# Attention scores of a head pair in one three-bank PSUM tile, with one maximum per head, from the 21st pair on

## The chip, the cores and the metric

The kernel runs on one core of one Trainium2 chip. The metric is device time in microseconds (us) of one launch; the result is the median of several launches.

## What is computed

Two layers of a diffusion backbone run over 1024 latent tokens of width 1024, beside 256 context tokens. Layer 0 mixes tokens with a gated MLP, layer 1 with windowed attention, and a ConvGLU feed-forward follows each. The change lies in the attention of layer 1: blocks of 128 queries, 16 heads of 64 dimensions, 4 key/value heads. Cut to what matters:

```python
scale = HEAD_DIM ** -0.5
for j in blocks:                        # 8 blocks of 128 queries
    s_lat = q[j] @ k[j-1 : j+2].T       # up to three key blocks
    s_lat = where(|q - k| <= 128, s_lat * scale, -inf)
    s_ctx = q[j] @ k_ctx.T * scale      # all 256 context keys
    p = softmax(concat(s_lat, s_ctx, sink))   # the sink column is dropped after
    out[j] = p_lat @ v[j-1 : j+2] + p_ctx @ v_ctx
y = out @ w_o
```

Blocks 1 to 6 have 384 local keys and 256 context keys (640 in all), blocks 0 and 7 have 256 and 256.

## The kernel before

One program is written as if for a single thread; a scheduling layer then places each engine's instructions in a fixed order and adds the semaphores. Every engine works through its queue in that order, so an instruction that waits holds up all that stand behind it on its engine. All instructions are recorded in one helper, so the profile gives L50 as the line of nearly everything; groups are told apart by the names of the tiles that they write and read.

Large matmuls are done in three passes of a high and a low part ("wh", "wl" and so on). Attention (`att_a`, `att_b`, `att_c`, lines 1876 to 1968) is a software pipeline over 64 pairs of heads, numbered i = 8 j + 2 g + pr for block j, key/value head g and pair pr. The loop at line 2028 issues, for each i, `att_a` of pair i (scores, maximum, softmax), `att_b` of pair i - 2 (transposes of the softmax weights) and `att_c` of pair i - 3 (weights times values). From i = 20 on it also weaves in steps of the output projection (`o_steps`, line 1970), by the table `sched`: six 512-column matmuls a step, named "wh,oc" in the profile.

- `att_a`: TensorE multiplies the queries of a head ("tmp") with the keys' high and low parts ("big"). The sign is folded in, so the maximum is a minimum. On VectorE a masked add with a running minimum (CUSTOM_DVE_ANT_0) moves scores from PSUM to SBUF, into `Pt` ("tmp" for the first head, "wl" for the second), and a READ_ACCUMULATOR writes the minimum to "sm". ScalarE then takes the exponential with that bias and adds up the row, VectorE takes the reciprocal, and GpSimd (POOL) multiplies.
- Pairs 8 to 23 are "merged": each head has its own two-bank tile `psA` with context and local scores side by side, six matmuls, and one VectorE operation over 640 columns.
- All other pairs put both heads' local scores in one `psA` tile (a bank each) and both heads' context scores in one bank `psB`: eight matmuls, then four VectorE operations, since a second one per head carries the minimum on over the context.
- `att_b`: ten 128-column transposes ("ident,tmp" and "ident,wl") into three `psB` banks; ScalarE casts a bank to "act" (high part), and VectorE subtracts to get the low part.
- `att_c`: ten 256-column matmuls ("act,y") into one `psB` bank, then a ScalarE copy and two VectorE adds into "row".

PSUM has eight banks: two buffers `psA` of two banks and four buffers `psB` of one, for the whole program. While an output projection is under way, one `psA` holds its sum `pacc` for eight steps, and scores have the other.

Of the kernel before, what the change touches and what calls it, by code (L numbers as in the profile page):

```python
# [10 lines left out]
F32 = mybir.dt.float32  # L11
F32R = mybir.dt.float32r
AF = mybir.ActivationFunctionType
ALU = mybir.AluOpType

P = 128
D = 1024
KD = D // P
# [14 lines left out]
def hybrid_kernel(  # L33
# [37 lines left out]
    open_pool("mix")  # L71
    ps = ctx.enter_context(tc.tile_pool(name="ps", bufs=1, space=bass.MemoryType.PSUM))
    dr = ctx.enter_context(tc.tile_pool(name="dr", bufs=1, space=bass.MemoryType.DRAM))
# [3 lines left out]
    def nm(s):  # L77
        uid[0] += 1
        return f"{s}_{uid[0]}"
# [43 lines left out]
    def t_sm(w=2):  # L123
        return sb.tile([P, w], F32, name=nm("sm"), tag="sm", bufs=24)
# [5 lines left out]
    def psA(shape=(P, 2, 512)):  # L130
        return ps.tile(list(shape), F32, name=nm("psA"), tag="psA", bufs=2)

    def psB(shape=(P, 512)):
        return ps.tile(list(shape), F32, name=nm("psB"), tag="psB", bufs=4)

# [43 lines left out]
    ones = ones_r.bitcast(F32)  # L179
    mhalf = const.tile([P, 1], F32, name="mhalf")  # L180
    G.memset(mhalf, -0.5)
    mone = const.tile([P, 2], F32, name="mone")
    G.memset(mone, -1.0)
# [242 lines left out]
    def tick():  # L426
        for gen in list(active):
            if next(gen, 1):
                active.remove(gen)
# [393 lines left out]
    def gmlp(si, hb, tiles, gate, extra, between, pre_last, on_flip=None, head=None, order=(0, 1, 2, 3, 4), mod=None):  # L823
        st = const.tile([P, 5, 24], F32, name=nm("st"))
        if head:
# [28 lines left out]
        rs, nmr = t_sm(5), t_sm(5)  # L854
        mv = t_sm(10).rearrange("p (i n) -> p i n", i=5)
        for i in range(5):
# [960 lines left out]
    def after_b(bi, u):  # L1817
# [9 lines left out]
        if bi == 2:  # L1827
# [5 lines left out]
            if u == 2:  # L1833
                q_prep(0, 1)

    maskw = const.tile([P, 640], F32, name="mask")
    G.memset(maskw, 0.0)
# [4 lines left out]
                    pattern=[[-1, 384]], channel_multiplier=1)  # L1842
    NM = 24
    snk = const.tile([P, NH], F32, name="snk")
# [28 lines left out]
    def merged(j, g, pr):  # L1873
        return 8 <= 8 * j + 2 * g + pr < NM

    def att_a(j, g, pr):
        k0, kts = geo[j]
# [9 lines left out]
        if merged(j, g, pr):  # L1887
            for h in range(2):
                lh = qs[:, 2 * pr + h, :]
                sl = psA()  # L1890
                for dst, c in ((sl[:, 0, 0:256], 1024), (sl[:, 0, 256:512], k0 * P), (sl[:, 1, 0:P], k0 * P + 256)):
                    n = dst.shape[-1]
                    T.matmul(dst, lh, KH[g][:, c:c + n], start=True, stop=False)
                    T.matmul(dst, lh, KL[g][:, c:c + n], start=False, stop=True)
                V.tensor_tensor_reduce(out=Pt[h][:, 0:NK], in0=sl.rearrange("p a b -> p (a b)")[:, 0:NK],
                                       in1=maskw[:, 0:NK], scale=1.0,
                                       scalar=nsnk[:, h0 + h:h0 + h + 1], op0=ALU.add, op1=ALU.min,
                                       accum_out=mx[:, h:h + 1])
            softmax(Pt, mx, es, dn, h0, NK)
            at[(j, g, pr)] = Pt  # L1900
            return
# [22 lines left out]
    def att_b(j, g, pr):  # L1924
        nk = len(geo[j][1])
        Pt = at[(j, g, pr)]
        PTh, PTl = t_act((P, 5, 2, P)), t_act((P, 5, 2, P))
        for a in range(0, nk, 2):
            n = min(2, nk - a)
            pt = psB((P, 2, 2, P))  # L1930
            for b in range(n):
                for h in range(2):
                    T.transpose(out=pt[:, b, h, :], in_=Pt[h][:, (a + b) * P:(a + b + 1) * P], identity=ident)
            S.copy(PTh[:, a:a + n], pt[:, 0:n])
            V.tensor_sub(PTl[:, a:a + n], pt[:, 0:n], PTh[:, a:a + n])
        at[(j, g, pr)] = (PTh, PTl)
# [3 lines left out]
    def att_c(j, g, pr):  # L1940
        kts = geo[j][1]
        nk = len(kts)
        if merged(j, g, pr):
            kts = kts[-2:] + kts[:-2]
# [25 lines left out]
    def o_steps(tiles):  # L1970
# [22 lines left out]
        for h in range(2):  # L1993
            pacc = psA()
            for k in range(KD):
                load(h * KD + k + 2)
                w, oc = wts.pop(h * KD + k), ocs.pop(h * KD + k)
                for i in range(nt):
                    hs = slice(i * P, (i + 1) * P)
                    mm3(pacc[:, i, :], oc[:, 0, hs], oc[:, 1, hs], w[:, 0], w[:, 1],  # L2000
                        k == 0, k == KD - 1)
                yield
            for i in range(nt):
                S.copy(ys[i][:, h * 512:(h + 1) * 512], pacc[:, i, :])
        for i in range(nt):
# [21 lines left out]
    n_pairs = len(pairs)  # L2027
    for i in range(n_pairs + LC):
        if i < n_pairs:
            j, g, pr = pairs[i]  # L2030
# [26 lines left out]
    while next(og, 1) is None:  # L2057
        tick()

    def last_o():  # L2060
# [20 lines left out]
    lat_ffn(1, 3, 5, halos, gate_of(1, 5), chain(last_o(), flushes(True)), ada_steps(1, 5, (0,), True))  # L2081
    stage_pool["guard"].__exit__(None, None, None)


# [40 lines left out]
```

## Time and profile before

| what | value |
|---|---|
| median of three runs | 2849.98 us (2846.95 to 2852.19) |
| the profiled execution, its own time | 2852.14 us |
| its span, first to last instruction | 2850.4 us |
| mean granted TensorE clock | 0.990 |
| TensorE matmul (PE) busy | 2735.4 us (96%) |
| VectorE (DVE) busy | 2218.6 us (78%) |
| ScalarE (ACT) busy | 1390.8 us (49%) |
| GpSimd (POOL) busy | 623.2 us (22%) |
| scores of pair 20 begin, last scores of pair 63 end | 1879 us, 2129 us |

How to read it: spans and starts count from the first instruction. A matmul's end is modelled, and neighbours overlap, so for TensorE the step from one start to the next says more than the duration. "PEld" is the weight load of a matmul. An entry "[1.29 <-DVE sm]" is idle time ahead of an instruction with the engine and tile that ended it.

### The profile page before, as it was taken

What the parts mean: (1) busy time and instruction counts of PE and PEld (TensorE: products, weight loads), DVE (VectorE), ACT (ScalarE), POOL (GpSimd) and SP (SyncE); (2) the same over time, 40 slices, a digit from 0 to 9 for tenths busy, and PEclk for the clock granted to TensorE, in tenths of its full rate; (3) what the DMA queues carried; (4) which work ended last, traced back from release to release, by engine and by line L of the source; (5) the groups of instructions that cost most, each with busy time, mean ns of one, the idle gap of its engine ahead of it and who ended that gap; (6) DMA issues with size and microseconds to landing.
All of it is one profiled execution on the core that took longest, in us unless ns stands there. A gap on an engine that the chain in (4) does not pass through costs nothing.

```text
span 2850.4 us, 40321 instructions
## 1 busy us (share of the span) xinstructions
PE 2735.4 (96%) x14570; PEld 2348.8 (82%) x14570; DVE 2218.6 (78%) x3466; ACT 1390.8 (49%) x2291; POOL 623.2 (22%) x806
## 2 busy tenths in 40 slices
PE   7999999999989999999999999899998999999998
PEld 5798887898879888888888788788887888888886
DVE  6567685687779898887786658898887788888776
ACT  4233243232367444455444545777876444445433
POOL 1064021260110122121000124543332122220000
PEclk9999999999999999999999999999999999999999
DMA  7785447554478345467845665347577355445753
GB/s 261 237 244 171 146 142 240 184 158 127 174 233 249 121 159 170 143 219 231 313 157 187 201 210 188 115 139 238 186 241 231 122 168 179 157 144 196 254 176 125
DMA packets 436335, 537.13 MB, mean 188 GB/s; under 512 B 20004, under 2 KB 300452, under 8 KB 436135
## 3 DMA queue, kind: packets, MB, share of 16 engines
q1 hardware_dynamic: 379575, 470.84, 51.5%
q10 hardware_dynamic: 55408, 59.52, 6.2%
q0 software_dynamic: 1152, 4.19, 0.4%
q8 instruction: 115, 1.88, 0.3%
q14 instruction: 85, 0.70, 0.1%
HBM read 414.40 MB, written 120.07 MB: 188 GB/s over the span
## 4 chain that ended last, share of the span: by engine, by line
PE 69%; DVE 12%; DMA 9%; ACT 4%; issue 4%; POOL 2%; SPq 1%; ACTq 0%; DVEq 0%; POOLq 0%
PE psB L50 52%; PE psA L50 17%; DVE row L50 3%; DMA raw<-in_ada_w_dram 3%; DVE wl L50 3%; DVE acc L50 1%; DVE tmp L50 1%; ACT wh L50 1%; DVE y L50 1%; ACT tmp L50 1%; DMA raw<-in_f_w_up_dram 1%; DMA xT<-row 1%; SPq L50 1%; POOL sm L50 1%; DVE act L50 1%
## 5 line engine op out<-in xcount | busy, mean ns | idle before, releaser
L50 PE MATMUL psB<-cmb,wh 128*128 128x512 f32 (+2 forms) x2584 | 750.5, 374 | 8.1 <-ACT row L50 5.6
L50 PEld LDWEIGHTS psB<-cmb,wh 128*128 128x128 f32 x2584 | 471.9, 188 | 99.2 <-ACT row L50 8.0
L50 PE MATMUL psB<-cmb,wl 128*128 128x512 f32 (+2 forms) x1292 | 482.9, 374 | 0.0
L50 ACT CAST wh<-raw 128x1024 fp32r<-128x1024 f32 (+1 forms) x313 | 265.2, 863 | 436.4 <-PE psB L50 173.6
L50 DVE TENSOR_TENSOR wl<-raw,wh 128x1024 fp32r<-128x1024 f32 (+1 forms) x313 | 308.9, 1002 | 97.2 <-ACT wh L50 95.5
L50 PEld LDWEIGHTS psB<-cmb,wl 128*128 128x128 f32 x1292 | 243.1, 188 | 43.6 <-DVE wl L50 0.2
L50 PE MATMUL psB<-wh,big 128*128 128x512 f32 x816 | 271.4, 399 | 4.0 <-ACT big L50 1.3
L50 ACT CAST wh<-row 128x1024 fp32r<-128x1024 f32 (+1 forms) x196 | 162.5, 834 | 189.9 <-DVE row L50 97.0
L50 PE MATMUL psB<-wh,act 128*128 128x512 f32 x640 | 200.2, 391 | 0.8 <-DVE tmp L50 0.8
L50 POOL TENSOR_TENSOR row<-raw,raw 128x512 f32<-128x512 f32 x44 | 73.2, 1664 | 572.2 <-DMA raw<-in_f_w_up_dram 516.6
L50 PE MATMUL psA<-big,wh 128*128 128x320 f32 x1024 | 194.4, 312 | 0.3 <-ACT row L50 0.3
L50 DVE TENSOR_TENSOR wl<-row,wh 128x1024 fp32r<-128x1024 f32 (+1 forms) x196 | 185.4, 949 | 11.8 <-ACT wh L50 11.8
L50 DVE SCALAR_TENSOR_TENSOR acc<-raw,ccols,acc 128x1024 f32<-128x1024 f32 x98 | 125.8, 1302 | 81.2 <-DMA raw<-in_ada_w_dram 81.1
L50 PEld LDWEIGHTS psB<-wh,big 128*128 128x128 f32 x816 | 154.7, 191 | 40.2 <-ACT big L50 2.4
L50 DVE SCALAR_TENSOR_TENSOR row<-row,cwcols,row 128x1024 f32<-128x1024 f32 (+2 forms) x142 | 150.8, 1062 | 39.2 <-ACT row L50 22.6
L50 ACT CAST ah<-raw 128x1024 fp32r<-128x1024 f32 x80 | 77.6, 974 | 202.2 <-PE psB L50 80.9
L50 POOL TENSOR_SCALAR row<-row,sm,sm 128x128 f32<-128x128 f32 x160 | 146.0, 926 | 114.0 <-DMA row<-vscr 63.3
L50 DVE TENSOR_TENSOR row<-row,row 128x512 f32<-128x512 f32 (+4 forms) x169 | 156.9, 932 | 17.3 <-DMA row<-actd 10.5
L50 PEld LDWEIGHTS psA<-big,wh 128*128 128x128 f32 x1024 | 160.9, 189 | 0.7 <-ACT row L50 0.5
L50 PE MATMUL psB<-wl,big 128*128 128x512 f32 x408 | 157.9, 397 | 0.6 <-DVE wl L50 0.6
L50 DVE TENSOR_TENSOR al<-raw,ah 128x1024 fp32r<-128x1024 f32 x80 | 90.3, 1128 | 71.4 <-ACT ah L50 71.1
L50 PE MATMUL psB<-row,wh 128*128 128x256 f32 x744 | 133.6, 283 | 9.5 <-ACT wh L50 7.5
(279 smaller groups left out, 6210.7 us busy)
## 6 DMA issues: line engine op xcount, KB each, us to landing
raw<-in_f_w_up_dram SPq DMA_DIRECT2D x121, 512.0 KB, 4.9
raw<-in_ada_w_dram SPq DMA_DIRECT2D x88, 512.0 KB, 4.4
raw<-in_a_w_in_dram SPq DMA_DIRECT2D x64, 512.0 KB, 4.6
wh<-woscr SPq DMA_DIRECT2D x48, 512.0 KB, 4.4
row<-actd SPq DMA_DIRECT2D x44, 512.0 KB, 5.3
actc<-row SPq DMA_DIRECT2D x44, 512.0 KB, 4.1
raw<-actc SPq DMA_DIRECT2D x40, 512.0 KB, 3.8
actd<-row SPq DMA_DIRECT2D x39, 512.0 KB, 2.6
```

The lines of the kernel that those rows point to most:

```text
L50: ins = fn(*a, **kw)
```

## The change

From pair 20 on (`NM` falls from 24 to 20, so merged pairs are 8 to 19) a pair is "joined": both heads' scores lie in one tile `psS` of three banks. The first head has its 384 local scores at the end of the first bank and its context in the first half of the middle bank; the second head has its context in the second half of the middle bank and its local scores in the third. Each head's 640 columns are so contiguous, and one VectorE operation takes them. The mask gains 256 zero columns at its end, and the transposes of the first head are read in an order that fits.

The PSUM pool is closed and reopened at i = 20 with other sizes: one `psS` (three banks), one `psO` (two banks, for the output projection's sum) and three `psB`. After the projection of the first six blocks it is reopened once more as at the start. The copies out of the projection's sum move into the step that ends it. Two constants now share a tile, and the statistics of layer 0 share another; near 170 us some small VectorE operations change places.

```diff
     def psA(shape=(P, 2, 512)):
-        return ps.tile(list(shape), F32, name=nm("psA"), tag="psA", bufs=2)
+        return banks_pool["pool"].tile(list(shape), F32, name=nm("psA"), tag="psA", bufs=2)
+
+    def psS():
+        return banks_pool["pool"].tile([P, 1536], F32, name=nm("psS"), tag="psS", bufs=1)
+
+    def psO():
+        return banks_pool["pool"].tile([P, 2, 512], F32, name=nm("psO"), tag="psO", bufs=1)
 
     def psB(shape=(P, 512)):
-        return ps.tile(list(shape), F32, name=nm("psB"), tag="psB", bufs=4)
+        return banks_pool["pool"].tile(list(shape), F32, name=nm("psB"), tag="psB", bufs=banks_pool["small"])
...
-    maskw = const.tile([P, 640], F32, name="mask")
+    maskw = const.tile([P, 896], F32, name="mask")
...
-    NM = 24
+    NM = 20
...
+    def joined(j, g, pr):
+        return 8 * j + 2 * g + pr >= NM
...
+        if joined(j, g, pr):
+            sl = psS()
+            for h in range(2):
+                lh = qs[:, 2 * pr + h, :]
+                local, o = (512 - NL, 512 - NL) if h == 0 and j < 7 else (512 * h + 512, 512 * h + 256)
+                context = 512 if h == 0 and j < 7 else 512 * h + 256
+                for c, k, n in ((local, k0 * P, NL), (context, 1024, 256)):
+                    T.matmul(sl[:, c:c + n], lh, KH[g][:, k:k + n], start=True, stop=False)
+                    T.matmul(sl[:, c:c + n], lh, KL[g][:, k:k + n], start=False, stop=True)
+                m = 256 if h == 0 and j < 7 else 0
+                V.tensor_tensor_reduce(out=Pt[h][:, 0:NK], in0=sl[:, o:o + NK], in1=maskw[:, m:m + NK], scale=1.0,
+                                       scalar=nsnk[:, h0 + h:h0 + h + 1], op0=ALU.add, op1=ALU.min,
+                                       accum_out=mx[:, h:h + 1])
+            softmax(Pt, mx, es, dn, h0, NK)
+            at[(j, g, pr)] = Pt
+            return
...
-            pacc = psA()
+            pacc = psO()
...
+                if k == KD - 1:
+                    for i in range(nt):
+                        S.copy(ys[i][:, h * 512:(h + 1) * 512], pacc[:, i, :])
                 yield
-            for i in range(nt):
-                S.copy(ys[i][:, h * 512:(h + 1) * 512], pacc[:, i, :])
...
+        if i == NM:
+            open_banks("ps2", reuse_waits="tile")
+            banks_pool["small"] = 3
...
+    open_banks("ps3", reuse_waits="tile")
```

What this does to the order of instructions is shown at one place, pair 32 and its neighbours, on the two engines that pass the scores on. First TensorE before: "psA" is the tile of local scores and "psB" with "big" that of the context, "tmp" behind "big" the queries; "ident" rows are the transposes of an earlier pair.

```order
L50 MATMUL psA_18022<-big_15607,tmp_17943 128x384
L50 MATMUL psA_18022<-big_15608,tmp_17943 128x384
L50 MATMUL psB_18023<-big_15607,tmp_17943 128x256
L50 MATMUL psB_18023<-big_15608,tmp_17943 128x256
L50 MATMUL psA_18022<-big_15607,tmp_17943 128x384
L50 MATMUL psA_18022<-big_15608,tmp_17943 128x384
L50 MATMUL psB_18023<-big_15607,tmp_17943 128x256
L50 MATMUL psB_18023<-big_15608,tmp_17943 128x256
L50 MATMUL psB_18043<-ident,tmp_17859 128x128
```

The same place on TensorE in the changed program, with the semaphores that instructions wait for; nine transposes (eight of them left out here) stand between the two heads.

```order
L50 MATMUL psS_17979<-big_15604,tmp_17903 128x384 [waits DVE_49]
L50 MATMUL psS_17979<-big_15605,tmp_17903 128x384
L50 MATMUL psS_17979<-big_15604,tmp_17903 128x256
L50 MATMUL psS_17979<-big_15605,tmp_17903 128x256
...
L50 MATMUL psS_17979<-big_15604,tmp_17903 128x384 [waits DVE_49]
L50 MATMUL psS_17979<-big_15605,tmp_17903 128x384
L50 MATMUL psS_17979<-big_15604,tmp_17903 128x256
L50 MATMUL psS_17979<-big_15605,tmp_17903 128x256
```

The eight matmuls came in one piece; now each head's four stand apart, and the second head's first matmul waits for VectorE. Then VectorE before, at the same pair ("ISA" with a mask is the masked minimum, "ISA sm" the read of the accumulator, "act" the low parts of an earlier pair's transposes):

```order
L50 ISA tmp_18018,sm_18016<-psA_18022,mask,nsnk 128x384
L50 ISA sm_18016 128x1
L50 ISA wl_18019,sm_18016<-psA_18022,mask,nsnk 128x384
L50 ISA sm_18016 128x1
L50 ISA tmp_18018,sm_18016<-psB_18023,mask,sm_18016 128x256
L50 ISA sm_18016 128x1
L50 ISA wl_18019,sm_18016<-psB_18023,mask,sm_18016 128x256
L50 ISA sm_18016 128x1
L50 TENSOR_TENSOR act_18042<-psB_18043,act_18041 128x512
```

and in the changed program:

```order
L50 ISA tmp_17975,sm_17973<-psS_17979,mask,nsnk 128x640
L50 ISA sm_17973 128x1
L50 TENSOR_TENSOR act_17996<-psB_17997,act_17995 128x512
L50 ISA wl_17976,sm_17973<-psS_17979,mask,nsnk 128x640
L50 ISA sm_17973 128x1
L50 TENSOR_TENSOR act_17996<-psB_18004,act_17995 128x512
```

Four minima and four reads became two and two, and a subtraction of the transposes moved in between the heads.

More of the change, by code (lines that the diff above doesn't have):

```diff
@@ L71, in hybrid_kernel, with open_banks @@
     open_pool("mix")
-    ps = ctx.enter_context(tc.tile_pool(name="ps", bufs=1, space=bass.MemoryType.PSUM))
+    banks_pool = {}
+    def open_banks(name, **kw):
+        if banks_pool:
+            banks_pool.pop("guard").__exit__(None, None, None)
+        banks_pool["guard"] = tc.tile_pool(name=name, bufs=1, space=bass.MemoryType.PSUM, **kw)
+        banks_pool["pool"] = banks_pool["guard"].__enter__()
+        banks_pool["small"] = 4
+    open_banks("ps")
     dr = ctx.enter_context(tc.tile_pool(name="dr", bufs=1, space=bass.MemoryType.DRAM))
@@ L179, in hybrid_kernel @@
     ones = ones_r.bitcast(F32)
-    mhalf = const.tile([P, 1], F32, name="mhalf")
+    powers = const.tile([P, 3], F32, name="powers")
+    mhalf, mone = powers[:, 0:1], powers[:, 1:3]
     G.memset(mhalf, -0.5)
-    mone = const.tile([P, 2], F32, name="mone")
     G.memset(mone, -1.0)
@@ L823, in gmlp @@
     def gmlp(si, hb, tiles, gate, extra, between, pre_last, on_flip=None, head=None, order=(0, 1, 2, 3, 4), mod=None):
-        st = const.tile([P, 5, 24], F32, name=nm("st"))
+        stats = const.tile([P, 184], F32, name=nm("st"), tag="st")
+        st = stats[:, 0:120].rearrange("p (i n) -> p i n", i=5)
         if head:
@@ L854, in gmlp @@
         rs, nmr = t_sm(5), t_sm(5)
-        mv = t_sm(10).rearrange("p (i n) -> p i n", i=5)
+        mv = stats[:, 120:130].rearrange("p (i n) -> p i n", i=5)
         for i in range(5):
@@ L1932, in att_b @@
                 for h in range(2):
-                    T.transpose(out=pt[:, b, h, :], in_=Pt[h][:, (a + b) * P:(a + b + 1) * P], identity=ident)
+                    c = (a + b + 3) % 5 if h == 0 and nk == 5 and joined(j, g, pr) else a + b
+                    T.transpose(out=pt[:, b, h, :], in_=Pt[h][:, c * P:(c + 1) * P], identity=ident)
             S.copy(PTh[:, a:a + n], pt[:, 0:n])
@@ L1942, in att_c @@
         nk = len(kts)
-        if merged(j, g, pr):
+        if merged(j, g, pr) or joined(j, g, pr):
             kts = kts[-2:] + kts[:-2]
@@ L2082, in hybrid_kernel @@
     stage_pool["guard"].__exit__(None, None, None)
+    banks_pool["guard"].__exit__(None, None, None)
 _INS = ['x', 'c', 'ctx', 'c_ctx', 'ada_w', 'ada_b', 'norm_g', 'a_w_in', 'a_ln_g', 'a_ln_b', 'a_w_s', 'a_b_s',
```

## Prediction

> **What bounds the kernel now.** I read the page's busy times first, then the stretch of the changed pairs.
>
> ```profile
> PE 2735.4 (96%) x14570; PEld 2348.8 (82%) x14570; DVE 2218.6 (78%) x3466; ACT 1390.8 (49%) x2291; POOL 623.2 (22%) x806
> ```
>
> TensorE is busy nearly throughout, so the kernel can only shrink where TensorE idles or does less. The next view cuts the stretch of pairs 20 to 63 into parts, with the busy time of each engine; its last row is the whole stretch, from a second answer.
>
> ```profile
> core 0: us, PE busy (x) PEld busy (x) DVE busy (x) ACT busy (x) POOL busy (x), PEclk, DMA share, GB/s
> 1879.00:1925.00 46.00, 43.16 (x301) 38.26 (x300) 43.65 (x130) 33.02 (x77) 21.23 (x24) 1.00 0.69 221
> 1925.00:1965.00 40.00, 39.44 (x275) 35.70 (x275) 35.14 (x127) 30.07 (x74) 12.55 (x18) 1.00 0.60 200
> 1965.00:1990.00 25.00, 19.70 (x116) 16.80 (x115) 18.66 (x53) 15.11 (x35) 5.85 (x10) 0.93 0.82 273
> 1990.00:2062.00 72.00, 70.41 (x502) 64.01 (x502) 63.53 (x232) 58.69 (x136) 26.45 (x36) 1.00 0.56 187
> 2062.00:2080.00 18.00, 15.43 (x87) 13.14 (x86) 14.82 (x39) 11.43 (x27) 4.62 (x8) 0.91 0.89 296
> 2080.00:2131.00 51.00, 50.50 (x363) 45.62 (x362) 44.26 (x168) 40.56 (x93) 17.95 (x26) 1.00 0.71 242
> ...
> 1879.00:2131.00 252.00, 238.63 (x1634) 213.53 (x1633) 220.07 (x744) 188.86 (x435) 88.64 (x120) 0.99 0.67 223
> ```
>
> TensorE is idle for 252.00 - 238.63 = 13.4 us of the stretch. In 1925 to 1965, 1990 to 2062 and 2080 to 2131, 163 us, it idles 0.56 + 1.59 + 0.50 = 2.65 us: there it sets the pace. The rest lies in three pieces, at the start, where VectorE is busy 43.65 of 46 us, and around 1975 and 2070. Who ended that idle time is told by the waits of TensorE over the stretch.
>
> ```profile
> PE psB L50 <- DVE sm L50: 4.8, 5, 1.6
> PE psA L50 <- DMA oc<-oscr: 2.6, 1, 2.6
> PE psA L50 <- DVE sm L50: 2.3, 4, 1.0
> PE psB L50 <- DVE act L50: 1.9, 3, 0.8
> PE psB L50 <- ACT tmp L50: 0.4, 2, 0.2
> PE psB L50 <- DVE row L50: 0.3, 1, 0.3
> ```
>
> "DVE sm" is the read of a maximum: a bank of scores came free only then. It accounts for 7.1 us, over half. The largest of these is not a score matmul but the values' product, which wanted a `psB` bank that scores still held:
>
> ```profile
> 2017.10 1.08 PE L50 MATMUL psB<-act,y 128*128 128x256 f32 x7 [1.57 <-DVE sm L50]
> ```
>
> **The change part by part.** First the work that VectorE is rid of. The rows of one pair as it is, a pair with 384 local keys:
>
> ```profile
> 1945.60 0.62 DVE L50 CUSTOM_DVE_ANT_0 tmp<-psA,mask,nsnk 128x384 f32<-128x384 f32 x1 [0.43 <-PE psA L50]
> 1946.14 0.08 DVE L50 DVE_READ_ACCUMULATOR2_ANT sm<- 128x1 f32 x1
> 1946.14 0.61 DVE L50 CUSTOM_DVE_ANT_0 wl<-psA,mask,nsnk 128x384 f32<-128x384 f32 x1
> ...
> 1946.68 0.48 DVE L50 CUSTOM_DVE_ANT_0 tmp<-psB,mask,sm 128x256 f32<-128x256 f32 x1
> ...
> 1947.08 0.48 DVE L50 CUSTOM_DVE_ANT_0 wl<-psB,mask,sm 128x256 f32<-128x256 f32 x1
> ...
> 1947.49 1.61 DVE L50 TENSOR_TENSOR act<-psB,act 128x512 fp32r<-128x512 f32 x3
> ```
>
> and of a merged pair, whose two operations have the form that all pairs now get:
>
> ```profile
> 1867.98 0.87 DVE L50 CUSTOM_DVE_ANT_0 tmp<-psA,mask,nsnk 128x640 f32<-128x640 f32 x1
> ...
> 1868.78 0.88 DVE L50 CUSTOM_DVE_ANT_0 wl<-psA,mask,nsnk 128x640 f32<-128x640 f32 x1
> ...
> 1869.59 0.21 DVE L50 COPY wl<-nsnk 128x1 f32<-128x1 f32 x2
> ```
>
> From start to start four operations take 1947.49 - 1945.60 = 1.89 us and two take 1869.59 - 1867.98 = 1.61 us, reads included. So 0.28 us goes with each of pairs 24 to 63. Pairs 56 to 63 have 512 columns: the step of 256 is 1947.08 - 1946.68 = 0.40 us and that of 384 0.54 us, which puts 512 at 0.67 us, and 4 x 0.40 - 2 x 0.67 is 0.26 us, much the same. In all 40 x 0.28 = 11.2 us of VectorE go. Pairs 20 to 23 had one operation a head already. This is a relief of VectorE, not of the path: where TensorE sets the pace it is worth nothing.
>
> TensorE's own work hardly changes. Pairs 24 to 63 keep eight matmuls of the same widths. Pairs 20 to 23 have eight in place of twelve, with the same 640 columns a head; twelve took 1.50 us in the first row below, and eight take 1945.79 - 1944.38 = 1.41 us in the two after it. At most 0.1 us a pair: I take 0.
>
> ```profile
> 1879.02 1.50 PE L50 MATMUL psA<-big,tmp 128*128 128x256 f32 x12
> 1881.51 0.78 PE L50 MATMUL psA<-big,tmp 128*128 128x256 f32 x5 [0.99 <-DVE sm L50]
> ...
> 1944.38 0.60 PE L50 MATMUL psA<-big,tmp 128*128 128x384 f32 x2
> ...
> 1945.39 0.40 PE L50 MATMUL psB<-big,tmp 128*128 128x256 f32 x2
> 1945.63 0.27 PE L50 MATMUL psB<-ident,tmp 128*128 128x128 f32 x1
> ...
> 1946.61 0.27 PE L50 MATMUL psB<-ident,wl 128*128 128x128 f32 x1
> ```
>
> The new wait is the heart of the change. All score matmuls of a pair could go in one piece; now the second head's wait until VectorE has read the first head's maximum, and the next pair's first head waits for the second's, as there is only one `psS`. Behind a waiting matmul stand the rest of the transposes, the values' product and the projection, so each such wait is TensorE's own time. The second row above prices it with nothing in between: the scores of pair 20 ended at 1880.52, the next could start 0.99 us later. The modelled end lies 1945.79 - 1945.63 = 0.16 us behind the slot of the next instruction, so the hand-over costs 1.15 us less the work that stands between. Ten transposes step over (1946.61 - 1945.63) / 9 x 10 = 1.09 us, nine over 0.98 and eight over 0.87. In the changed order only 15 of the 44 first hand-overs have such little work between: one has five transposes (0.60 us short), six have nine (0.17 each), four have ten (0.06 each), three of the 512-column pairs have eight (their maximum is 0.13 us shorter, so 1.02 us is needed and each is 0.15 short) and one has enough. Sum: 0.60 + 1.02 + 0.24 + 0.45 = 2.3 us. Eight more have 1.2 to 1.35 us between and would wait only if VectorE came late. The second hand-over has the values' product and mostly projection work between, but VectorE takes a subtraction of an earlier pair first; I add 1.0 us for the few with the product alone. So 3.3 us; the lower bound is 0 if the queue's own gaps swallow them, the upper one stands with the rivals.
>
> [...]
>
> What goes in return: the 2.3 us of "psA <- DVE sm" vanish as such, since that hand-over is now the one just priced. Of the 4.8 us of "psB <- DVE sm", `psB` no longer holds scores, but with three buffers the values' product takes the bank of that pair's first transposes, whose subtraction follows the first head's maximum on VectorE. That is 0.81 us for the maximum and 0.68 us for the subtraction
>
> ```profile
> L50 DVE TENSOR_TENSOR act<-psB,act 128x512 fp32r<-128x512 f32 x88 | 57.4, 684 | 2.1 <-ACT act L50 1.9
> ```
>
> against 1.89 us, so 0.40 us sooner in each of five waits: 2.0 us. The three waits on "DVE act" come 0.28 us sooner each, 0.8 us. The wait on the load of "oc" stays at 2.6 us, because it hangs on a store and a load of the projection's input.
>
> Parts with one answer, taken at 0: the wider memset on POOL at the start, the shared constants and statistics (the same operations, a few swapped), and swaps of a few loads on SP's queue. The copies out of `psO` are the same pieces on ScalarE,
>
> ```profile
> L50 ACT COPY acc<-psA 128x512 f32<-128x512 f32 x10 | 6.0, 595 | 0.1
> ```
>
> two to a half of the sum; matmuls of attention stand ahead of the next half's, and without that cover five turns would cost up to 1.2 us each. Reopening the pool lets a tile wait for the tiles it overlays only, once each way.
>
> The clock: TensorE had 0.93 and 0.91 of it in the two stretches with the most idle, 25 x 0.07 = 1.8 us and 18 x 0.09 = 1.6 us lost, and 1.00 elsewhere. I leave both. [...]
>
> Sum against the profiled execution: 2852.14 - 2.3 - 2.0 - 0.8 + 3.3 = 2850.3 us. That execution lies 2.2 us above the median, 2849.98, so on the median's scale 2848 us. The three runs spread over 5 us, about 0.2%, which is what counts as a difference here.
>
> **The rivals.** Faster: VectorE's lateness, not the hand-over, is what TensorE pays for, and 11.2 us less of it clears the idle. Of the 13.4 us of idle all but the load's 2.6 us and 0.8 us of small gaps go, which is 10.0 us, and 1.6 us of clock, less 1.0 us of second hand-overs. 2852.14 - 10.6 = 2841.5, or 2839 on the median's scale. For it speaks the first part, where VectorE is busy 43.65 of 46 us; against it that 163 us of the stretch hold 2.65 us of idle.
>
> Slower: the hand-overs bind. VectorE is busy 220 of 252 us, so a first maximum seldom starts at once; if it starts 0.3 to 0.4 us late on average, 23 hand-overs cost about 0.5 us each. 11.5 + 1.0 - 2.3 - 2.0 - 0.8 = +7.4, so 2859.5, or 2857 on the median's scale. For it speaks that the old order issued both heads at once and idled little. It decides from (2.3 + 2.0 + 0.8 - 1.0) / 23 = 0.18 us a hand-over on.
>
> No change: the waits just pass to another tile of the same late engine, since three `psB` are left; 2850.
>
> **How the numbers follow.** My forecast has a chance of 0.42, with 2842 to 2852 as its own range; the faster rival 0.22, the slower 0.18, no change 0.18. Faster by over 0.2% (below 2844.3) takes 0.13 of the forecast, 0.20 of the faster rival and 0.01 of no change: 0.34. Slower takes 0.16 of its rival and 0.02 of no change: 0.18. The rest, 0.48, is the same. The range reaches from just below the faster rival, 2837, to 2858.
>
> **What would show it.** VectorE's busy time should fall by some 11 us by steps (more by durations), with 80 masked minima less. Ahead of "psS" matmuls there should be idle time ended by "DVE sm", a few us in all, and none of it ahead of "psB". If TensorE's idle in the stretch falls to about 4 us, the faster rival holds; if "psS <- DVE sm" sums to 8 us or more, the slower one. A change of more than 3 us outside 1879 to 2190 us would mean that I looked in the wrong place.

## The result and the profile after

The changed kernel takes 2868.22 us (median of 4 runs, 2866.80 to 2870.07), the kernel before 2850.51 us beside it (2846.95 to 2852.19). The ratio is 1.0065, with a 95% interval of 1.005 to 1.008: 17.7 us slower. Its profiled execution took 2866.80 us, with a span of 2865.0 us; the two traces are thus 14.7 us apart and show a little less than the medians.

From the page of the changed kernel, the busy times:

```profile
PE 2745.7 (96%) x14554; PEld 2355.8 (82%) x14554; DVE 2210.7 (77%) x3306; ACT 1392.4 (49%) x2291; POOL 620.2 (22%) x806
```

VectorE has 160 instructions less, the 80 minima and 80 reads, and 7.9 us less to do. It did not help. The stretch of pairs 20 to 63, cut at about the same places of the work as for the kernel before (the last row, from a second answer, is the whole):

```profile
core 0: us, PE busy (x) PEld busy (x) DVE busy (x) ACT busy (x) POOL busy (x), PEclk, DMA share, GB/s
1876.00:1927.00 51.00, 45.84 (x301) 40.01 (x298) 45.37 (x122) 34.84 (x80) 20.54 (x25) 0.97 0.67 213
1927.00:1970.00 43.00, 41.70 (x284) 37.01 (x282) 34.19 (x97) 31.57 (x74) 13.75 (x18) 1.00 0.54 173
1970.00:1992.00 22.00, 17.42 (x98) 14.93 (x99) 16.75 (x39) 13.88 (x33) 5.72 (x8) 0.92 0.93 319
1992.00:2068.00 76.00, 73.09 (x506) 64.67 (x504) 62.27 (x179) 59.47 (x138) 27.51 (x36) 1.00 0.55 179
2068.00:2090.00 22.00, 18.83 (x101) 16.48 (x102) 15.74 (x37) 11.93 (x27) 7.03 (x9) 0.84 0.91 300
2090.00:2142.00 52.00, 50.80 (x350) 44.43 (x350) 40.50 (x118) 40.08 (x93) 17.64 (x26) 1.00 0.61 204
...
1876.00:2142.00 266.00, 247.69 (x1634) 217.51 (x1632) 214.82 (x588) 191.78 (x441) 92.19 (x121) 0.97 0.64 211
```

The stretch grew from 252 to 266 us. TensorE idles 18.3 us in it, where it was 13.4; VectorE idles more than before, 51 us against 32. The waits of TensorE over the same stretch:

```profile
PE psO L50 <- DMA oc<-oscr: 4.8, 2, 2.7
PE psS L50 <- DVE sm L50: 3.7, 7, 1.0
PE psS L50 <- DVE row L50: 3.4, 1, 3.4
PE psB L50 <- ACT tmp L50: 2.4, 4, 1.0
PE psB L50 <- DVE act L50: 1.6, 4, 0.7
PE psB L50 <- DVE row L50: 0.8, 3, 0.3
PE psB L50 <- ACT act L50: 0.3, 1, 0.3
```

"psB <- DVE sm" and "psA <- DVE sm", 7.1 us before, are gone. In their place stand `psS` (7.1 us), a second wait for "oc" and small waits of `psB`. But idle time explains only 4.9 of 14 us, since a matmul's modelled end covers short waits (0.17 us of one in the pair shown below, where its row has no idle time). So all matmul starts of the loop (from the values' product of pair 16 to that of pair 63) were taken instead: the step from each start to the next, less about the shortest step that a matmul of its width has in these two traces at a granted clock of 1.00 (0.226 us for 512 columns, 0.170 for 384, 0.1135 for 256, 0.109 for a transpose; gaps under 0.05 us left out). What is left, by the matmul that came late; steps of about twice their length have a row of their own:

| us of gaps ahead of | before | after |
|---|---|---|
| scores | 6.2 | 17.2 |
| transposes and values' products (`psB`) | 12.2 | 14.7 |
| the projection | 7.1 | 8.1 |
| steps of about twice their length | 8.2 | 7.6 |
| sum | 33.7 | 47.6 |
| this part of the loop | 260.1 | 273.6 |

Without the gaps, both kernels take the same to within 0.4 us (260.1 - 33.7 and 273.6 - 47.6). So the 13.5 us are gaps, most of them (11.0 us) ahead of scores. The row of doubled steps is not the clock alone: by the granted clock in the two views, the stretch lost 25 x 0.07 + 18 x 0.09 = 3.4 us before and 51 x 0.03 + 22 x 0.08 + 22 x 0.16 = 6.8 us after. At least 4.8 of the 8.2 us before are therefore short waits, and the clock takes about 3.4 us more than it did.

The gaps are of three kinds. The first is one wait, at the reopened pool. TensorE of the changed kernel:

```profile
1876.19 1.43 PE L50 MATMUL psB<-act,y 128*128 128x256 f32 x10
1881.00 1.41 PE L50 MATMUL psS<-big,tmp 128*128 128x384 f32 x4 [3.38 <-DVE row L50]
1882.21 1.27 PE L50 MATMUL psB<-ident,tmp 128*128 128x128 f32 x5
```

and VectorE, which had these ahead of the two adds into "row" that set the bank free:

```profile
1877.14 1.22 DVE L50 TENSOR_TENSOR row<-row,row 128x1024 fp32r<-128x1024 f32 x1
...
1878.75 1.62 DVE L50 TENSOR_TENSOR act<-psB,act 128x512 fp32r<-128x512 f32 x3 [0.19 <-ACT act L50]
1880.29 0.57 DVE L50 TENSOR_TENSOR row<-psB,tmp 64x128 f32<-64x128 f32 x2
```

Before, the scores of pair 20 followed the values' product at once, without a wait (the row at 1879.02 us in the prediction). Now they lie over banks whose last user is the values' product just ended, and wait for its copy and adds. Five transposes behind the wait take 1.27 us, where 4 x 0.109 + 0.27 = 0.71 us is usual: the granted clock was 0.50 from 1881 to 1884 us. The second kind is the hand-over between a pair's heads. TensorE in one pair, with nine transposes between the heads (seven left out):

```profile
1947.03 0.84 PE L50 MATMUL psS<-big,tmp 128*128 128x384 f32 x4
1947.70 0.27 PE L50 MATMUL psB<-ident,tmp 128*128 128x128 f32 x1
...
1948.57 0.27 PE L50 MATMUL psB<-ident,tmp 128*128 128x128 f32 x1
1948.85 0.85 PE L50 MATMUL psS<-big,tmp 128*128 128x384 f32 x4
```

and VectorE at that time:

```profile
1947.90 0.88 DVE L50 CUSTOM_DVE_ANT_0 tmp<-psS,mask,nsnk 128x640 f32<-128x640 f32 x1 [0.68 <-PE psS L50]
1948.71 0.08 DVE L50 DVE_READ_ACCUMULATOR2_ANT sm<- 128x1 f32 x1
```

The step behind the last transpose is 0.28 us in place of 0.11: the second head waited 0.17 us for the first maximum. The row of the matmuls shows no idle time there, but the row of their weight loads does:

```profile
1948.85 0.65 PEld L50 LDWEIGHTS psS<-big,tmp 128*128 128x128 f32 x4 [0.24 <-DVE sm L50]
```

In the whole stretch the weight loads of scores waited for a maximum 31 times, where the list of the matmuls' waits has 7 times and 3.7 us. A load waits ahead of its matmul (0.24 us above, where the step was 0.17 us late), so not all of this is TensorE's loss:

```profile
PEld psS L50 <- DVE sm L50: 12.4, 31, 1.4
```

The 17.2 us split into 6.0 us at second heads (29 of 44 come late), 6.0 us at first heads, 3.55 of it at the reopening, and 5.2 us of short gaps among the four matmuls of a head. The hand-over has a part in these too: behind a second head that came late, the step from its first matmul to its second is 0.11 us too long (median), behind one in time 0.01. The third kind is the short waits of transposes for a `psB`.

### The profile page after: what moved, and what is told of

It reads as the page before. It is cut to its first block, busy times and chain, and to the rows that moved or that the text cites. A ratio compares the mean times of both kernels' runs of the same rounds, so it can differ in the third digit from the quotient of the medians.

```text
span 2865.0 us, 40095 instructions
## 1 busy us (share of the span) xinstructions
PE 2745.7 (96%) x14554; PEld 2355.8 (82%) x14554; DVE 2210.7 (77%) x3306; ACT 1392.4 (49%) x2291; POOL 620.2 (22%) x806
## 5 line engine op out<-in xcount | busy, mean ns | idle before, releaser
L50 DVE TENSOR_TENSOR row<-row,row 128x512 f32<-128x512 f32 (+4 forms) x169 | 157.7, 937 | 23.4 <-DMA row<-actd 11.1
L50 POOL TENSOR_TENSOR sm<-sm,powers 128x1 f32<-128x1 f32 (+2 forms) x38 | 32.2, 848 | 547.7 <-DVE sm L50 546.4
```

The source lines that it names most:

```text
L50: ins = fn(*a, **kw)
```

## The experiments

The theories: the reopened pool (R), the hand-over between the heads (H), the lost fourth `psB` (B), the second wait for "oc" with its clock (O). Differences are to the median of the kernel before in the same comparison, on the same chip; an interval is that of the ratio. All edits are to the changed kernel unless said.

### The pools with the old scores

```diff
-            V.tensor_tensor_reduce(out=Pt[h][:, 0:NK], in0=sl[:, o:o + NK], ...
+            bank = psS()
+            sl = bank[:, 0:1024].rearrange("p (h n) -> p h n", h=2)
+            sc = bank[:, 1024:1536].rearrange("p (h n) -> p h n", h=2)
```

> The changed kernel's three PSUM pools, with the old form of the scores in them: from pair 20 on the three-bank tile holds both heads' local scores in two banks and both contexts in the third, all eight matmuls first, then four masked minima. (Pairs 20 to 23 thereby go from two minima to four, 1.1 us more of VectorE.) If the cost lies in the pools (the reopened banks, one score tile at a time, three small banks for four, a bank pair of its own for the projection), this stays near the changed kernel, 2866 to 2874 us, since the saved VectorE time is given back as well. If it lies in the joined form itself (the second head's matmuls wait for the first head's maximum), it comes to 2854 to 2858 us.

Measured: 2868.90 us against 2850.71, +18.2 us (1.0046 to 1.0075), as foreseen if the pools are the cost. But its largest wait, over the loop, is one that the changed kernel hardly has:

```profile
PE psB L50 <- DVE act L50: 19.0, 15, 2.3
```

With VectorE's old work, three `psB` come free too late. What the pools cost depends on the form of the scores, so the two had to be taken apart further.

### Other banks for the score tile

```diff
             banks_pool["small"] = 3
+            psB(), psO(), psS()
```

> The changed kernel with the score tile on banks 5 to 7 in place of 0 to 2, so that at pair 20 it lies over old psA banks, which the maxima of pair 19 set free, and not over old psB banks, which the last adds of a values' product set free. If reopening the pool costs what the trace shows there (TensorE idle 1.4 us, and 3.5 us behind after pair 20 against 1.5 us ahead before it), some 3 us go: 2865 us, 2863.5 to 2866.5. If VectorE is simply late at pair 20 whatever bank it is, the time stays within 1 us of 2868.

Measured: 2869.28 us, +18.6 (1.0052 to 1.0079). No gain. The scores no longer wait at pair 20, but the first transposes do, since their `psB` now lies in the bank of the last values' product:

```profile
PE psB L50 <- DVE row L50: 3.7, 4, 2.8
```

One of the two has to take the bank that is freed last.

### All eight matmuls first

```diff
                     T.matmul(sl[:, c:c + n], lh, KL[g][:, k:k + n], start=False, stop=True)
+            for h in range(2):
+                o = 512 - NL if h == 0 and j < 7 else 512 * h + 256
                 m = 256 if h == 0 and j < 7 else 0
```

> The changed kernel with all eight score matmuls of a joined pair ahead of its two minima: the second head no longer waits for the first head's maximum; the next pair's matmuls wait for both. If the hand-over between the heads is the cost (psS waits for VectorE of 3.7 us, and what the order lost by it), the time falls by 4 to 9 us to 2859 to 2864. If one score tile at a time is the cost, the wait only moves to the next pair's first matmul: 2866 to 2872.

Measured: 2865.67 us, +15.0 (1.0041 to 1.0070). That is 2.7 us less than the changed kernel, each against its own before, within the intervals, and short of the 4 to 9 us of H. The gaps of the second heads are gone, but those of the first heads rose from 6.0 to 14.5 us, at 22 of 44 turns: the wait moved to the next pair.

### The projection one step later

```diff
         load(1)
         yield
+        yield
...
-    sched = ((20, 36, 0, 19), (36, 52, 19, 19), (52, 66, 38, 19))
+    sched = ((20, 36, 0, 20), (36, 52, 20, 20), (52, 66, 40, 20))
```

> The changed kernel with the output projection's matmuls one step later behind their first loads (one empty step after them, the same last step). If the two waits for oc (2.8 us at 1977 and 2.3 us at 2074) and the half clock behind them (3.4 and 6.8 us at half speed) are what the change lost, they go: 5.1 us of idle and up to 5 us of clock, 2858 to 2863 us. If the projection's matmuls only uncover a late VectorE elsewhere, it stays at 2866 to 2870.

Measured: 2869.17 us, +18.5 (1.0047 to 1.0079). It removed nothing: its trace still shows 5.1 us of waiting for "oc" in two places, since the scheduler set the projection's matmuls nearly where they were (the first begins at 1885.2 us in place of 1885.4). So O was not tested by it.

### Reopening alone

The kernel before, with `open_banks` added and nothing else:

```diff
     for i in range(n_pairs + LC):
+        if i == 20:
+            open_banks("ps2", reuse_waits="tile")
...
     while next(og, 1) is None:
         tick()
+    open_banks("ps3", reuse_waits="tile")
```

> The kernel before, with its PSUM pool closed and opened again at pair 20 and after the pair loop, as in the changed kernel, but with the same tiles in it (psA twice, psB four times) and all scores in the old forms. If reopening by itself costs what the trace of the changed kernel shows at pair 20 (3.4 us of waiting for VectorE's adds) and the late part of the kernel does not catch it up, 2853 to 2856 us; if the old kernel's own stalls a little later swallow it, as they seem to (the changed kernel is level again by pair 22), 2849 to 2852.

Measured: 2856.79 us against 2849.58, +7.2 (1.0015 to 1.0033). R is real, and larger than its wait. The clock in 1878 to 1886 us, first in the kernel before, then in this one:

```profile
1878.00:1886.00 8.00, 6.58 (x54) 6.09 (x53) 7.38 (x20) 6.21 (x17) 1.57 (x2) 1.00 0.64 187
```

```profile
1878.00:1886.00 8.00, 5.96 (x28) 6.00 (x29) 4.85 (x13) 3.52 (x10) 1.26 (x2) 0.60 0.79 247
```

The wait of 3.4 us is followed by 8 x 0.40 = 3.2 us lost to the clock; the changed kernel had 0.79 there, 1.7 us.

### Three psB with the old scores

The run with reopening alone, with one line more:

```diff
+            banks_pool["small"] = 3
```

> The same as the one before it, with three psB in place of four from pair 20 to the end of the loop, psA kept at two and the old forms of the scores kept. If the lost bank is the main cost of the change, this alone reaches 2860 us or more (in the run with the changed pools and the old four minima, psB waited 19 us for VectorE's subtractions); if the single score tile is, it stays within 3 us of the run with the reopened pool alone.

Measured: 2874.86 us, +25.3 (1.0071 to 1.0097), 18.1 us more than the run before it. B is large with the old scores, which also keep a `psB` for the context. The changed kernel, with as few `psB` but no scores in them, stands 7.6 us better (25.3 against 17.7).

### Joined later

```diff
-    NM = 20
+    NM, NJ = 24, 36
...
-        return 8 * j + 2 * g + pr >= NM
+        return 8 * j + 2 * g + pr >= NJ
```

> The changed kernel with the joined form and its pools only from pair 36 on, the kernel before up to there (merged to pair 23, separate to pair 35, the projection's first sum in psA). 28 of the 44 pairs keep the change. If the loss is a price per pair (the hand-over), 28/44 of 17 us stay: 2860 to 2862. If it is the reopening at pair 20, where VectorE was late (43.7 of 46 us busy), most of it goes: 2851 to 2855.

Measured: 2862.92 us, +13.3 (1.0032 to 1.0057).

With 52 for 36:

```diff
+    NM, NJ = 24, 52
```

> The same from pair 52 on, 12 of the 44 pairs. Price per pair: 12/44 of 17 us, 2854 to 2856. Reopening as such, wherever it is: 2854 to 2857 with no difference between the two. Neither, the lateness at pair 20 alone: 2849 to 2852.

Measured: 2857.66 us, +8.1 (1.0016 to 1.0034). 44, 28 and 12 pairs cost 17.7, 13.3 and 8.1 us: about 0.3 us a pair, and some 4 to 5 us however few there are. So there is a price per pair beside a fixed one, and neither reading alone fits. Whether the fixed part is the reopening stays open for pairs 36 and 52: the waits for "row" there are 1.2 us, and a later run, with the old scores, puts reopening at pair 36 at no cost.

### Reopening, taken apart

The kernel before with the second reopening alone:

```diff
     while next(og, 1) is None:
         tick()
+    open_banks("ps3", reuse_waits="tile")
```

> The kernel before with its PSUM pool reopened only after the pair loop, with the same tiles, and not at pair 20. Every run with reopened pools so far lost 2.4 to 4.9 us between the last values' product and the end of the kernel. If the reopening at the end is the reason, this is 2 to 5 us slower than before, 2852 to 2855; if only what the loop left behind (its delay, the clock) is, it stays within 1.5 us of 2849.6.

Measured: 2848.83 us against 2849.24, -0.4 (0.9989 to 1.0010). The reopening at the end costs nothing. The kernel before with both, and a tile asked for first so that all lie over their own kind:

```diff
             open_banks("ps2", reuse_waits="tile")
+            psB()
```

> The kernel before with both reopenings, as in the run with the reopened pool alone (2856.8 us), but with an empty psB asked for first, so that psB keeps banks 0 to 3 and psA 4 to 7 and each new tile lies over an old one of its own kind. There, psA lay over the old psB banks and its first matmul waited 3.4 us for VectorE's adds. If it is the swap of the banks that costs, 2849 to 2852; if the reopening itself (the new tile waits for all that its bank held, wherever it lies), 2855 to 2858.

Measured: 2857.73 us, +8.5 (1.0016 to 1.0036): no cheaper than reopening over other banks. The waits between 1875 and 1960 us:

```profile
PE psB L50 <- DVE act L50: 3.3, 2, 3.0
PE psB L50 <- DVE row L50: 2.1, 1, 2.1
```

No score waits long. The 2.1 us are the first transposes behind the last values' product, waiting for its adds: again a new tile meets the bank that is freed last. The 3.0 us have another cause. VectorE itself stood still ahead of the subtraction that the next values' product waited for:

```profile
1886.18 0.69 DVE L50 TENSOR_TENSOR raw<-raw,row 128x512 f32<-128x512 f32 x1 [3.40 <-DMA raw<-qraw]
```

It waited for a load. In the kernel before, VectorE came to this step at 1889.78 us, behind the subtractions that here stand after it, and did not wait; with reopening alone it is early as well, and waited 0.85 us. So reopening also brought another order on VectorE, and what this order and the banks cost each is not separated.

### The other edits alone

No pair joined, no pool reopened:

```diff
-    NM = 20
+    NM, NJ = 24, 999
```

> The changed kernel with no pair joined and no pool reopened: merged to pair 23, separate after it, psA twice and psB four times throughout. What is left of the change are the shared constants and statistics, the wider mask and the projection's copies moved into its last step. In all runs with these edits the values' products come 0.4 to 3.9 us sooner at the start of the pair loop, apart from one that is 2.4 us late, and in the run joined from pair 52 on they were 7 us ahead by pair 36, with no wait for oc there. If that is from these edits, 2843 to 2847 us; if it is chance in the clock and in the queues, 2849 to 2851.

Measured: 2847.39 us, -1.9 (0.9983 to 1.0003). No difference that can be measured. The 7 us ahead in the trace of the run joined from pair 52 on do not stand for its median: that execution took 2853.2 us, 4.4 less than it.

### The fourth psB given back

```diff
-        return ...tile([P, 2, 512], F32, name=nm("psO"), ...
+        return ...tile([P, 2, 256], F32, name=nm("psO"), ...
...
-            banks_pool["small"] = 3
```

> The changed kernel with the projection summed in quarters of 256 columns in place of halves of 512: its psO takes one bank, and psB keeps four from pair 20 on. Its matmuls are twice as many at half the width, and its input oc is loaded twice as often. If the lost fourth bank is what the changed kernel pays for (18 us in the old forms of the scores), 2855 to 2860 us; if the single score tile and its hand-over are, 2866 to 2870, or more if the added loads are late.

Measured: 2876.00 us, +26.8 (1.0075 to 1.0105). The loads came too late, and the run says little on B:

```profile
PE psO L50 <- DMA wh<-woscr: 5.3, 4, 3.5
PE psO L50 <- issue: 4.8, 1, 4.8
PE psO L50 <- DMA oc<-oscr: 4.0, 2, 2.3
```

With the weights of two steps in one load:

```diff
-            w = t_w("wh", F32R, (P, 2, 512))
+            w = t_w("wh", F32R, (P, 2, 2, 256))
```

> The changed kernel with four psB again, as in the run before it, but with the quarters' weights loaded for two steps of the sum at a time: one step of the projection has the work and the lead that it has in the changed kernel, and only its input oc is loaded twice as often. In the run before, the waits ahead of transposes and values' products came to 6.3 us against 14.6 us in the changed kernel, and the late loads cost more than that. If the lost bank is what the joined form pays for, and the loads are in time, 2857 to 2862 us; if the hand-over through the one score tile is, 2865 to 2870.

Measured: 2868.60 us against 2851.34, +17.3 (1.0045 to 1.0074). No gain from the bank alone. Gaps ahead of `psB` users fell from 14.7 to 7.5 us, and came back at the second heads (10.5 us) and at "oc" (9.1 us of waits, 4.8 in the changed kernel), each of these waits with a lower clock behind it (0.92, 0.86 and 0.89 in the stretches below). And with the order of the third run:

```diff
+            for h in range(2):
+                o = 512 - NL if h == 0 and j < 7 else 512 * h + 256
```

> The first run of this call, with all eight score matmuls ahead of both minima as well. If what is left after the fourth bank is the hand-over between a pair's heads, 3 to 6 us less than that run; if it is the one score tile, within 2 us of it or more.

Measured: 2852.88 us, +1.5 (0.9998 to 1.0015), 15.7 us less than the run without that order. Its gaps: scores 11.2 us (3.6 of them the reopening), `psB` users 11.1, projection 5.2. Either edit alone was worth 0 to 3 us, both together 16:

| us above the kernel before | second head waits | all eight first |
|---|---|---|
| three `psB` | +17.7 | +15.0 |
| four `psB` | +17.3 | +1.5 |

Not all of the 15.7 us lie at the heads. The waits for "oc" fell from 9.1 to 3.5 us, and the clock behind them came back; first the run in which the second head waits, then the one with all eight first:

```profile
1925.00:1970.00 45.00, 41.07 (x305) 39.40 (x304) 33.05 (x95) 28.80 (x71) 14.15 (x18) 0.92 0.70 232
1970.00:1995.00 25.00, 18.61 (x128) 17.76 (x127) 17.04 (x41) 16.14 (x39) 6.21 (x10) 0.86 0.71 232
2065.00:2095.00 30.00, 24.57 (x174) 23.49 (x174) 21.84 (x51) 20.93 (x45) 10.06 (x15) 0.89 0.72 230
```

```profile
1925.00:1970.00 45.00, 42.37 (x342) 41.23 (x341) 37.68 (x105) 32.85 (x79) 15.57 (x20) 1.00 0.76 249
1970.00:1995.00 25.00, 21.35 (x167) 20.05 (x166) 22.52 (x57) 20.55 (x50) 11.50 (x18) 1.00 0.98 327
2065.00:2095.00 30.00, 25.43 (x200) 23.86 (x201) 25.59 (x67) 23.41 (x55) 12.33 (x20) 1.00 0.88 304
```

That is up to 45 x 0.08 + 25 x 0.14 + 30 x 0.11 = 10.4 us of clock (less where TensorE was waiting meanwhile), and 5.6 us of waits for the load. At the heads, the second head's 10.5 us went, but the next pair's first heads and the users of `psB` (7.5 to 11.1 us) took part of it back. Why less time was lost to the loads is not shown, so how much of the 16 us belongs to hand-over and bank, and how much to O, stays open.

### Where the reopening costs

The kernel before, its pool reopened at pair 36 and at the end:

```diff
-        if i == 20:
+        if i == 36:
```

> The kernel before with its pool reopened at pair 36 and at the end, the same tiles in it. At pair 20 that cost 7 to 8 us, whichever banks the new tiles got. If the price is that VectorE is late at pair 20, 2849 to 2852 us; if a reopened pool has it anywhere in the loop, 2855 to 2858.

Measured: 2849.31 us against 2851.34, -2.0 (0.9988 to 1.0007). It costs nothing there, though the wait exists:

```profile
PE psA L50 <- DVE row L50: 1.9, 1, 1.9
PE psB L50 <- DVE sm L50: 1.9, 1, 1.9
```

Here TensorE of the kernel before waited for "oc" anyway (2.6 us); in this run no wait for "oc" is listed at that place. It seems that a wait took the place of another.

### All of it from 36 and from 16 on

The kernel of +1.5 us, with the joined form and the reopening at pair 36:

```diff
-    NM = 20
+    NM, NJ = 24, 36
...
-            pacc = psO()
+            pacc = psO() if "own" in banks_pool else psA()[:, 0, :].rearrange("p (i n) -> p i n", i=2)
```

> The run with four psB and all eight matmuls first (2852.9 us), with its reopening and the joined form only from pair 36 on; up to there the forms of the kernel before, and the projection in quarters all along, its sum in one bank of a psA. Reopening at 36 cost nothing in the kernel before. If the price at pair 20 is what holds the run back, it goes and this is the fastest, 2843 to 2848 us; if the joined form's gain between pairs 20 and 36 (about 6 us in the trace of that run) is worth as much as the price, 2849 to 2853.

Measured: 2859.18 us against 2852.24, +6.9 (1.0010 to 1.0033), against all that was expected. Its executions lie in two groups, six from 2851 to 2857 us and six from 2861 to 2865; the profiled one took 2852.6, so what the others lose is not in the trace. And from pair 16 on:

```diff
-    NM = 20
+    NM = 16
```

> The same kernel with the reopening and the joined form from pair 16 on, before the projection's first step, the merged form for pairs 8 to 15. If the price of reopening belongs to pair 20 alone (a row of 1024 stands ahead of the adds on VectorE there), it goes: 2844 to 2849 us. If it is met wherever the last values' product ends just ahead of the reopening and nothing else fills TensorE, it stays, with four more pairs joined: 2851 to 2856.

Measured: 2856.57 us, +4.3 (1.0004 to 1.0022). The wait is there, shorter, and the clock holds:

```profile
PE psS L50 <- DVE row L50: 2.4, 1, 2.4
```

```profile
1858.00:1866.00 8.00, 5.57 (x46) 5.39 (x46) 5.59 (x17) 5.14 (x16) 5.11 (x9) 1.00 0.02 5
1866.00:1874.00 8.00, 7.74 (x63) 7.46 (x62) 7.64 (x22) 7.44 (x19) 3.56 (x6) 1.00 0.00 0
```

Its profiled execution took 2851.3 us, 5.3 less than the median, so what the others lose may not be in the trace. No version with joined pairs beats the kernel before.

### What two minima are worth

The kernel of +1.5 us with the old four minima in its tile:

```diff
-            sl = psS()
+            bank = psS()
+            sl = bank[:, 0:1024].rearrange("p (h n) -> p h n", h=2)
+            sc = bank[:, 1024:1536].rearrange("p (h n) -> p h n", h=2)
```

> The run with four psB and all eight matmuls first (2852.9 us), with the old four minima of a pair on the same three banks in place of two: pools, projection and order of the matmuls stay, VectorE has 0.28 us more to do for each of pairs 24 to 63 and 0.56 us or so more for pairs 20 to 23, 12 to 13 us in all. If VectorE's relief is what the joined form gives, a good part of that comes back on TensorE: 2858 to 2868 us. If the relief is off the path, 2851 to 2856.

Measured: 2862.72 us against 2852.41, +10.3 (1.0029 to 1.0060), 8.8 us more than with two. VectorE's busy time in 1876 to 2142 us, first with two minima, then with four:

```profile
1876.00:2142.00 266.00, 244.53 (x1967) 236.70 (x1965) 220.41 (x601) 200.52 (x470) 90.41 (x126) 0.99 0.81 266
```

```profile
1876.00:2142.00 266.00, 244.22 (x1942) 238.95 (x1941) 227.82 (x771) 194.69 (x456) 93.72 (x123) 0.97 0.80 259
```

VectorE's busy time differs by 7.4 us, the median by 8.8: in these pools the joined form is worth on TensorE about what it takes off VectorE. That the two are so near may be chance, since the granted clock fell as well, from 0.99 to 0.97 (266 x 0.02 = 5.3 us), and the scores also lie otherwise in their banks.

## Why the prediction was wrong, point by point

It said 2848 us; 2868 were measured, above its range. The step that failed first is one that the sum put at nothing: reopening the pool, which alone measured +7.2 us. The second is the balance of the new waits: the sum had a charge of 3.3 us for the hand-overs against a gain of 2.3 + 2.0 + 0.8 us, where the trace shows more waiting at both. How the rest of the 17.7 us divides is only in part shown.

- **"Reopening the pool lets a tile wait for the tiles it overlays only, once each way."** Once, but for 3.4 us at pair 20, with 1.7 us (changed kernel) or 3.2 us (reopening alone) of half clock behind it: 7.2 and 8.5 us in the two runs that only reopen, 3 us of wait in the second being VectorE's late load. The end costs nothing, as said. What was missed is that in every run reopened inside the loop something at once waited for the last values' product ("row", 1.2 to 3.4 us), and that at pair 20 VectorE had 3 us of other work ahead of freeing it.
- **The hand-overs, 3.3 us.** The mechanism was right: the 0.17 us behind nine transposes is found to the digit. The size was not: 29 second heads came late in place of 15, 6.0 us in place of 2.3, and the first heads lost 2.4 us beside the reopening, where 1.0 was put. With the 2.3 us of "psA" that were to vanish, gaps ahead of scores should have grown by 1.0 us; they grew by 11.0, of which the reopening is 3.55.
- **`psB`, a gain of 2.8 us.** It became a loss: gaps of 14.7 us against 12.2. The prediction gave `psB` credit for the scores that left it, with VectorE 0.40 us sooner at each wait, and did not charge that three banks are freed by the same VectorE as four. With the fourth bank back the gaps are 7.5 us, a gain of 4.7 in place of 2.8 (11.1 us with all eight matmuls first).
- **The terms added up as if each stood alone.** The table of four shows that they do not. Take away the hand-over, and the next pair waits instead; give back the bank, and the second head still waits. With both edits most of the loss is gone, but part of that came by way of the loads of "oc" and the clock, so why the two edits help each other is not shown.
- **VectorE's relief, "not of the path".** Not so in the new pools: with one score tile and four `psB`, two minima fewer a pair were worth 8.8 us, so they stand on TensorE's path there. In busy time VectorE lost 7.9 us, where 11 were worked out by steps.
- **TensorE's work, the constants, the moved copies, at 0.** Right: equal sums of steps, and -1.9 us for those edits alone, not told from 0.
- **The wait for "oc", "stays at 2.6 us".** There are two now, 4.8 us. What that is worth by itself stays open, as the run that was to remove them did not; the gaps ahead of the projection grew by only 1.0 us, but behind the second of the waits the clock was 0.84 over 22 us, 3.5 us, where the kernel before lost 1.6 there.
- **The clock, left as it was.** It doubled its price in the stretch, from 3.4 to 6.8 us: 1.5 us more at pair 20, where 1.00 fell to 0.79, and 1.9 us more around 2075. That a shorter idle near 2070 gives back the 1.6 us of clock that the faster rival counts on was the author's estimate, and no run shows it by itself. The nearest is the run of +1.5 us: its waits for "oc" were at most 1.5 us, and its clock was 1.00 from 2065 to 2095 us.

Of the signs to look for, "psS <- DVE sm" came to 3.7 us, below the 8 us that were to prove the slower rival. Its side was right and its mechanism is part of the cause, but its test looked at the waits of the matmuls, and most of the hand-over shows only in those of the weight loads, 12.4 us, or from start to start. Behind 2190 us the changed kernel loses some more: at the first feed-forward matmul it is 10.2 us behind, at the end 14.6. By the prediction's last sign, more than 3 us out there, the stretch does not hold all of the loss. But two runs that are not slower also lose between the same points (6.1 us with the reopening at the end, 2.2 with the other edits alone), so this is not told from chance in single executions.

## What to carry to other kernels

A tile that merges two saves an operation and lengthens the time that its banks are held; count what else those banks were for, and what can stand between one use and the next, before the saving is counted. Two limits can hide each other, so an edit that lifts one may show nothing: try both together, and look which waits then went. Read the waits of the weight loads beside those of the matmuls. Where a pool is rebuilt in the middle of a full pipeline, try the seam where the engine waits anyway: with the old scores it cost nothing there, though with the joined form at the same pair the kernel was still 6.9 us slower.

## What the runs showed of the hardware

Some long waits of TensorE cost more than themselves in these runs, where the granted clock was lower behind them. Behind 3.4 us at pair 20 the clock was 0.79 over 8 us in the changed kernel, and 0.60 in the run with reopening alone. It was 0.50 from 1880.7 to 1884.0 us in the first. In the second, 0.60 and then 0.98 over the next 8 us come to 6.7 us at 0.50, and its transposes from 1883.71 to 1885.42 us step 0.21 us, where 0.11 is usual. So the same wait of 3.38 us cost 8 x 0.21 = 1.7 us once and 8 x 0.40 = 3.2 us the other time. Behind 2.4 us, in the run joined from pair 16 on, the clock stayed at 1.00. But shorter waits were not free of it in every run: behind the 2.6 us of the kernel before the clock was 0.93 over 25 us, and in the run reopened at pair 36 two waits of 1.9 us close together stand in

```profile
1960.00:1985.00 25.00, 21.20 (x129) 18.99 (x129) 20.36 (x58) 17.13 (x40) 8.00 (x10) 0.86 0.80 264
```

which is 25 x 0.14 = 3.5 us of clock.
